# A running product begun one memory head later, and a weight product made ahead of the last column tile

## The chip, the cores and the metric

The kernel runs on one core of a Trainium2 chip. The metric is the device time of one execution in microseconds (us): the median of three runs of the kernel before is 1121.86 us, from 1120.22 to 1121.92. The core has five engines that work through instruction queues of their own: TensorE (PE; its weight loads are shown apart as PEld), VectorE (DVE), ScalarE (ACT), GpSimd (POOL) and SyncE (SP), which issues the loads here.

## What is computed

One hybrid decoder layer on 512 tokens of width 2048, in float32. A conditioning vector gives shift, scale and gate (adaLN); the normalised input goes through one wide projection whose columns feed two groups; both results go through an output projection, are multiplied by the gate and added to the input.

```python
mod = jax.nn.silu(cf) @ w_ada[l] + b_ada[l]
shift, scale, gate = jnp.split(mod, 3, axis=-1)
h = rmsnorm(h_res, ln_g[l]) * (1.0 + scale[:, None]) + shift[:, None]
p = h @ w_in[l] + b_in[l]
...
y_m = mlstm_group(m_x, m_v, m_o, m_z, m_i, m_f, ...)   # 4 memory heads of 256
y_n = nsa_group(n_q, n_kc, n_vc, n_ks, n_vs, n_kw, n_vw, n_g, n_z, ...)  # attention, 4 groups
y = jnp.concatenate([y_m, y_n], axis=-1) @ w_out[l]
h_res = h_res + gate[:, None] * y
```

A memory head convolves m_x over time, makes q and k from the same 256 columns xc by two weight matrices (`q = xch @ wq`, `k = xch @ wk`), and uses the products q k^T under a decay mask to weight v; the result is normalised and multiplied by a sigmoid of m_o and a silu of m_z.

## The kernel before

Activations lie transposed in SBUF: 16 tiles of 128 columns by 512 tokens. To keep float32 precision each operand is split into a high part and a remainder, and each product is three matmuls (high by high, high by low, low by high). The stages follow each other: adaLN and the first column tiles (to 132 us of the span), projections and compression (to 262), attention in four groups with the projections of later column tiles in between (to about 625), four memory heads (to 940), and the output projection (to the end).

`proj(name)` (L286 to L304) makes one column tile of 128 columns: two loads of 512 KB on SP (L292), four weight splits, and 48 matmuls of 512 columns (L298 to L300). A split (L117 to L128) is a cast on ACT (L123, the name ends in h) and a subtraction (L126, the name ends in l), which POOL does while `pat` is "p" (all of attention and head 0) and DVE while it is "v" (afterwards). The tiles are named mx, mv, mo and mz with a number, two of each for one head: mz2 and mz3 belong to head 1. `head_prep(hd)` makes the mx, mv and mz tiles of a head; `memory_head(hd)` does the rest with the mo tiles. The calls are: head_prep(0), conv(2), conv(3), mz_prep(1), and then memory_head(hd) and head_prep(hd + 1) in turn, so mz3 is the last tile ahead of head 0.

In memory_head the two weight matrices are multiplied with each other first: wqk = wq wk^T, 12 matmuls of 256 columns (L721 to L723). ACT casts the product to ah (L727), DVE makes the remainder al (L728), and 12 matmuls give qk = xc times it (L734 to L736). Then come the scores s, the decay weights, the output h and the mo tiles.

`gate_columns` (L809) is the gate's part of adaLN: 4 runs of 16 steps, each with a load of 256 KB on SP (adag, L814) and one DVE instruction that adds a weighted row block to gacc (L817 for the first step of a run, L819 for the others). It is a generator in the list `side_work`; each proj takes two steps from it after either half of its tile.

The instructions are put in order by a scheduler that works from program order and a timeline of its own, under the limits of slot pools: three slots for loaded weights ("raw"), four each for high parts ("whi", also ah) and remainders ("wlo", also al), two PSUM tiles "sc" shared by attention's scores ss and sw, wqk, qk and s. So what is written early can come late on an engine, and each engine then runs its own queue strictly in that order. The names of attention: ss and sw are scores of the selected and the window branch, ep and ec their exponentials (L549 on ACT, after a reduction L542 on DVE), tps, tpw and tpc transposes on PE, phs, phw and phc casts on ACT, pls and plw remainders on DVE, o the output products (L574, L580, L581). Bias, tanh and product of an mz tile are ym and th (L676, L678 on ACT, L679 on DVE).

Of the kernel before, what the change touches and what calls it, by code (L numbers as in the profile page):

```python
# [10 lines left out]
F32 = mybir.dt.float32  # L11
# [75 lines left out]
def layer_kernel(ctx: ExitStack, tc: tile.TileContext, x, cols, ada, ada_g, w_ko, w_tiles,  # L87
# [198 lines left out]
    def proj(name, tag="pj"):  # L286

        ti = TIDX[name] - NKO
        ps = psb(tag, f"pj_{name}")
        for hf in range(2):  # L290
            raw = raw_tile(f"w_{name}_{hf}")
            nc.sync.dma_start(raw, w_tiles[ti, hf])  # L292
            for q in range(2):
                wh, wl = split(raw[:, q * 512:(q + 1) * 512], 512, f"w_{name}_{hf}{q}")
                for j in range(4):
                    k = hf * 8 + q * 4 + j
                    c = slice(j * P, (j + 1) * P)
                    pe.matmul(ps, wh[:, c], hhi[k], start=(k == 0), stop=False)  # L298
                    pe.matmul(ps, wh[:, c], hlo[k], start=False, stop=False)  # L299
                    pe.matmul(ps, wl[:, c], hhi[k], start=False, stop=(k == KT - 1))  # L300
            if side_work:
                for _ in range(SIDE):
                    next(side_work[0], None)
        return ps  # L304

    side_work = []
    SIDE = 2

    def bcol(name):
# [353 lines left out]
        sc.activation(xc[i], acc, AF.Tanh, scale=0.5)  # L663
        ve.scalar_tensor_tensor(xc[i], xc[i], 1.0, acc, op0=ALU.add, op1=ALU.mult)

    def mz_prep(hd):

        tag = ("v", "kh", "kl", "v")[hd]
        shape = [P, 1056] if tag[0] == "k" else [P, 2 * T]
        y2 = na.tile(shape, F32, tag=tag, name=f"ym{hd}", bufs=2)  # L670
        for e in range(2):
            i = 2 * hd + e
            nm = f"mz{i}"
            ps = proj(nm)
            ym[i] = y2[:, e * T:(e + 1) * T]
            sc.activation(ym[i], ps, AF.Identity, bias=bcol(nm))  # L676
            th = tmp(f"th{i}")
            sc.activation(th, ps, AF.Tanh, bias=bhalf[:, TIDX[nm]:TIDX[nm] + 1], scale=0.5)  # L678
            ve.scalar_tensor_tensor(ym[i], th, 1.0, ym[i], op0=ALU.add, op1=ALU.mult)  # L679

    def mv_prep(hd):
        vh = na.tile([P, 1056], F32R, tag="kh", name=f"mvh{hd}", bufs=2)[:, :1032].rearrange("p (a b) -> p a b", b=258)
        vl = na.tile([P, 1056], F32R, tag="kl", name=f"mvl{hd}", bufs=2)[:, :1032].rearrange("p (a b) -> p a b", b=258)
        ve.tensor_copy(vh[:, :, 256:258], ones[:, 0:8].rearrange("p (a b) -> p a b", b=2))
        ve.tensor_copy(vl[:, :, 256:258], zero[:, 0:8].rearrange("p (a b) -> p a b", b=2))
        for e in range(2):
            nm = f"mv{2 * hd + e}"
            ps = proj(nm)
            vr = tmp(f"vr_{nm}")
            sc.activation(vr, ps, AF.Identity, bias=bcol(nm))  # L690
            tp = psb("tp", f"vtp_{nm}")
            for t in range(NT):
                pe.transpose(tp[:, t * P:(t + 1) * P], vr[:, t * P:(t + 1) * P], ident)
            tv = tp.rearrange("p (t d) -> p t d", d=P)
            c = slice(e * P, (e + 1) * P)
            sc.copy(vh[:, :, c], tv)
            ve.tensor_sub(vl[:, :, c], tv, vh[:, :, c].bitcast(F32))
        return vh, vl

    def memory_head(hd, vh, vl):  # L700
        def btile(name):
            return na.tile([P, 640], F32R, tag="bias", name=f"{name}{hd}", bufs=4)
        def etile(name):
            return na.tile([P, T], F32R, tag="ep", name=f"{name}{hd}", bufs=8)
        xh, xl = [etile(f"xh{e}") for e in range(2)], [etile(f"xl{e}") for e in range(2)]
        for e in range(2):
            sc.copy(xh[e], xc[2 * hd + e])
            ve.tensor_sub(xl[e], xc[2 * hd + e], xh[e].bitcast(F32))

        wt = []  # L710
        for w in range(2):
# [14 lines left out]
        s = 1.0 / 64  # L726
        sc.activation(ah, ps, AF.Copy, scale=s)  # L727
        ve.scalar_tensor_tensor(al, ps, s, ah.bitcast(F32), op0=ALU.mult, op1=ALU.subtract)  # L728
        qh, ql = [etile(f"qh{e}") for e in range(2)], [etile(f"ql{e}") for e in range(2)]
        for e in range(2):  # L730
            ps = psb("sc", f"qk{hd}{e}")
            for d in range(2):
                c = slice(d * 256 + e * P, d * 256 + (e + 1) * P)
                pe.matmul(ps, ah[:, c], xh[d], start=(d == 0), stop=False)  # L734
                pe.matmul(ps, ah[:, c], xl[d], start=False, stop=False)
                pe.matmul(ps, al[:, c], xh[d], start=False, stop=(d == 1))  # L736
            sc.copy(qh[e], ps)
            ve.tensor_sub(ql[e], ps, qh[e].bitcast(F32))
        rb = psb("ms", f"rb{hd}")
# [57 lines left out]
    def head_prep(hd):  # L797
# [2 lines left out]
            conv(2 * hd + 1)  # L800
        vv = mv_prep(hd)
        if hd != 1:
            mz_prep(hd)
        return vv


# [33 lines left out]
    vv = head_prep(0)  # L840
    conv(2)
    conv(3)
    mz_prep(1)
    for hd in range(MH):
        memory_head(hd, *vv)
        if hd == 0:
            pat[0] = "v"
            side_work.append(gate_columns())
        if hd + 1 < MH:
            vv = head_prep(hd + 1)  # L850
# [224 lines left out]
```

## Time and profile before

| what | value |
|---|---|
| runs | 1121.86, 1120.22, 1121.92 us |
| the profiled execution | 1121.27 us |
| its span, first to last instruction | 1119.5 us |
| mean granted clock of PE | 0.996 of 2.4 GHz |
| PE busy / PEld busy | 1091.5 us (98%) / 904.8 us (81%) |
| DVE / ACT / POOL busy | 692.9 / 547.2 / 207.8 us |
| chain that ended last, share on PE | 93% |

The profile is one execution. Its times run from the first instruction. A busy time of an engine in a window tells how much it worked there, a wait of an engine names the instruction that it was released by, and a timeline row gives start and length of one instruction. Instructions overlap a little in an engine, so the cost of one in a row of many is the distance between two starts.

### The profile page before, as it was taken

How to read it: one execution, taken by the hardware profiler on the slowest of the kernel's cores; microseconds unless marked ns; L12 is line 12 of the kernel's file. 1: busy time of each engine (PE TensorE's matmuls, PEld its weight loads, DVE VectorE, ACT ScalarE, POOL GpSimd, SP SyncE). 2: the span in 40 equal slices, each digit the busy share in tenths (PEclk: the TensorE clock that was granted, in tenths of full speed). 3: DMA queues.
4: the chain of work that ended last, by engine and by line, in shares of the span. 5: the costliest groups of instructions: out<-in, count | busy, mean ns of one | idle time of the engine just before them, and what ended most of it. 6: DMA issues, size and time to landing. Idle time of an engine off the chain costs nothing.

```text
span 1119.5 us, 18333 instructions
## 1 busy us (share of the span) xinstructions
PE 1091.5 (98%) x6754; PEld 904.8 (81%) x6754; DVE 692.9 (62%) x1739; ACT 547.2 (49%) x1235; POOL 207.8 (19%) x192
## 2 busy tenths in 40 slices
PE   5999999999999999999999899999999999999997
PEld 4777788888888887888788688888888888888896
DVE  6767466226667658666866985588568367445273
ACT  6333452346666668666656744333433264323242
POOL 1000300433335335333532320000010000000000
PEclk9999999999999999999999999999999999999999
DMA  9999424231211211121122443148426222443334
GB/s 375 406 403 379 158 95 135 92 132 60 72 57 57 75 58 58 57 76 57 57 67 66 151 137 108 66 165 277 133 76 207 95 76 84 142 149 131 108 113 160
DMA packets 49362, 150.30 MB, mean 134 GB/s; under 512 B 5876, under 2 KB 7796, under 8 KB 48760
## 3 DMA queue, kind: packets, MB, share of 16 engines
q1 hardware_dynamic: 49272, 149.13, 38.4%
q8 instruction: 53, 0.87, 0.3%
q14 instruction: 37, 0.30, 0.1%
HBM read 144.91 MB, written 4.19 MB: 133 GB/s over the span
## 4 chain that ended last, share of the span: by engine, by line
PE 93%; DVE 3%; ACT 2%; DMA 1%; issue 0%; POOL 0%; ACTq 0%; POOLq 0%; SPq 0%; DVEq 0%
PE ko L263 7%; PE po L945 5%; PE po L946 5%; PE po L947 5%; PE pj_mx L298 3%; PE pj_mx L299 3%; PE pj_mv L300 3%; PE pj_mv L298 3%; PE pj_mx L300 3%; PE pj_mv L299 3%; PE pj_q L298 3%; PE pj_mz L298 3%; PE pj_q L300 3%; PE pj_q L299 3%; PE pj_mz L299 3%; PE pj_mz L300 3%
## 5 line engine op out<-in xcount | busy, mean ns | idle before, releaser
L549 ACT ACTIVATE ep<-ep,nm 128x512 f32<-128x512 f32 (+3 forms) x128 | 71.4, 559 | 28.3 <-DVE nm L542 27.6
L780 POOL TENSOR_TENSOR sm<-sm,mhalf 128x1 f32<-128x1 f32 x16 | 12.0, 760 | 250.3 <-DVE sm L779 149.3
L819 DVE SCALAR_TENSOR_TENSOR gacc<-adag,sil,gacc 128x512 f32<-128x512 f32 x60 | 48.3, 807 | 6.5 <-DMA adag<-in_dram 5.8
L542 DVE CUSTOM_DVE_ANT_0 ep<-sw,bias 128x512 f32<-128x512 f32 (+3 forms) x64 | 29.8, 484 | 19.8 <-PE sw L617 12.4
L223 ACT ACTIVATE hhi<-xts,md 128x512 fp32r<-128x512 f32 x16 | 13.1, 817 | 57.9 <-DVE md L213 57.9
L542 DVE CUSTOM_DVE_ANT_0 ep<-ss,bias 128x512 f32<-128x512 f32 (+3 forms) x64 | 30.5, 486 | 17.4 <-PE tps L568 11.5
L562 DVE TENSOR_SCALAR ep<-ep,ff 128x512 f32<-128x512 f32 (+3 forms) x80 | 36.8, 508 | 0.6
L197 DVE SCALAR_TENSOR_TENSOR acc<-ada,sil,acc 128x256 f32<-128x256 f32 x75 | 36.1, 481 | 1.6
L579 DVE TENSOR_TENSOR pls<-tps,phs 128x512 fp32r<-128x512 f32 x40 | 27.2, 686 | 15.1 <-ACT phs L578 14.6
L907 POOL TENSOR_TENSOR rf<-rf,mhalf 128x1 f32<-128x1 f32 x4 | 2.2, 550 | 177.5 <-ACT tz L900 162.1
L579 DVE TENSOR_TENSOR plw<-tpw,phw 128x512 fp32r<-128x512 f32 x40 | 27.1, 682 | 7.4 <-ACT phw L578 7.1
L529 POOL TENSOR_SCALAR bias<-ct 128x640 f32<-128x640 f32 x16 | 29.6, 1854 | 3.2 <-DVE nm L542 2.2
L206 PEld LDWEIGHTS gp<-ada,cb 128*32 128x32 f32 x1328 | 20.1, 109 | 11.6 <-issue 6.4
L578 ACT CAST phw<-tpw 128x512 fp32r<-128x512 f32 x40 | 22.5, 581 | 11.7 <-PE tpw L568 9.3
L578 ACT CAST phs<-tps 128x512 fp32r<-128x512 f32 x40 | 23.0, 582 | 9.5 <-PE o L574 5.0
L549 ACT ACTIVATE ec<-ec,nm 128x32 f32<-128x32 f32 x64 | 20.2, 315 | 14.6 <-DVE nm L542 14.3
L560 ACT ACTIVATE ep<-ep,ff 128x512 f32<-128x512 f32 (+3 forms) x48 | 23.6, 553 | 7.5 <-DVE ff L554 7.2
L568 PE MATMUL tpw<-ct,ep 128*128 128x128 f32 x160 | 25.7, 272 | 0.1
L568 PE MATMUL tps<-ct,ep 128*128 128x128 f32 x160 | 25.5, 273 | 0.1
L206 PE MATMUL gp<-ada,cb 128*32 128x64 f32 x1328 | 25.6, 221 | 0.0
L568 PEld LDWEIGHTS tps<-ct,ep 128*128 128x128 f32 x160 | 20.1, 140 | 5.8 <-DVE ep L562 0.7
L549 ACT ACTIVATION_READ_ACCUMULATOR ep<-ep,nm 128x1 f32 x128 | 24.2, 189 | 0.0
(1097 smaller groups left out, 3800.1 us busy)
## 6 DMA issues: line engine op xcount, KB each, us to landing
ada<-in_dram SPq DMA_DIRECT2D x64, 512.0 KB, 7.5
adag<-in_dram SPq DMA_DIRECT2D x64, 256.0 KB, 3.9
wo<-in_dram SPq DMA_DIRECT2D x32, 512.0 KB, 3.3
w_q<-in_dram SPq DMA_DIRECT2D x16, 512.0 KB, 3.5
w_mx<-in_dram SPq DMA_DIRECT2D x16, 512.0 KB, 3.5
w_mv<-in_dram SPq DMA_DIRECT2D x16, 512.0 KB, 3.5
w_mz<-in_dram SPq DMA_DIRECT2D x16, 512.0 KB, 3.6
w_mo<-in_dram SPq DMA_DIRECT2D x16, 512.0 KB, 3.5
```

Of the source, the lines that this page charges most:

```text
L263: pe.matmul(ko_ps[j], (wl if p == 1 else wh)[:, c], (hlo if p == 2 else hhi)[k], start=(k == 0 and p == 0), stop=(k == KT - 1 and p == 2))
L298: pe.matmul(ps, wh[:, c], hhi[k], start=(k == 0), stop=False)
L299: pe.matmul(ps, wh[:, c], hlo[k], start=False, stop=False)
L300: pe.matmul(ps, wl[:, c], hhi[k], start=False, stop=(k == KT - 1))
L542: ve.tensor_tensor_reduce(dst, src, bs, -0.125, 3.0e38, ALU.add, ALU.min, nm[:, c:c + 1])
L549: sc.activation(tiles[hd], tiles[hd], AF.Exp, bias=nm[:, 4 * br + hd:4 * br + hd + 1], scale=-1.0, accum_out=zz[:, 4 * br + hd:4 * br + hd ...
L568: pe.transpose(tp[0:rows, hd * P:(hd + 1) * P], srcs[hd], ident)
L579: ve.tensor_sub(pl[0:rows, :], tp[0:rows, :], ph[0:rows, :].bitcast(F32))
L819: ve.scalar_tensor_tensor(acc, raw, w, acc, op0=ALU.mult, op1=ALU.add)
L945: pe.matmul(pss[i][:, :cn], yh[k][:, t], wh[:, c], start=f0, stop=False)
L946: pe.matmul(pss[i][:, :cn], yh[k][:, t], wl[:, c], start=False, stop=False)
L947: pe.matmul(pss[i][:, :cn], yl[k][:, t], wh[:, c], start=False, stop=l0)
```

## The change

Two things are edited. The generator of the gate's running product is appended to the side work after head 1 instead of after head 0, so its 64 steps are taken by the tiles of heads 2 and 3. And the weight product of a head is a function of its own, `weight_product(hd)`, which is called ahead of the last column tile that precedes the head: for head 0 ahead of mz3, for head 1 ahead of mv3, for heads 2 and 3 ahead of mz5 and mz7. What uses it, the qk matmuls, is ordered behind the last matmul of the last projection by `tc.issue_after`. In the new kernel the line numbers from L301 on are one higher, from L700 on they differ more.

```diff
-                    pe.matmul(ps, wl[:, c], hhi[k], start=False, stop=(k == KT - 1))
+                    last_proj[0] = pe.matmul(ps, wl[:, c], hhi[k], start=False, stop=(k == KT - 1)).ins
...
-    def mz_prep(hd):
+    def mz_prep(hd, head=None):
...
+            if e == 1 and head is not None:
+                weight_product(head)
             ps = proj(nm)
...
             nm = f"mv{2 * hd + e}"
+            if e == 1 and hd == 1:
+                weight_product(1)
             ps = proj(nm)
...
+    aqk = {}
+
+    def weight_product(hd):
...
         sc.activation(ah, ps, AF.Copy, scale=s)
         ve.scalar_tensor_tensor(al, ps, s, ah.bitcast(F32), op0=ALU.mult, op1=ALU.subtract)
+        aqk[hd] = ah, al
...
+        ah, al = aqk.pop(hd)
+        before = last_proj[0]
         qh, ql = [etile(f"qh{e}") for e in range(2)], [etile(f"ql{e}") for e in range(2)]
         for e in range(2):
             ps = psb("sc", f"qk{hd}{e}")
-            for d in range(2):
...
+            with tc.issue_after(before):
+                for d in range(2):
...
-            mz_prep(hd)
+            mz_prep(hd, hd if hd else None)
...
-    mz_prep(1)
+    mz_prep(1, 0)
     for hd in range(MH):
         memory_head(hd, *vv)
         if hd == 0:
             pat[0] = "v"
+        if hd == 1:
             side_work.append(gate_columns())
```

The scheduler turns this into another order on each engine. On PE, at the end of mz2 (pj_mz_6837; hhi and hlo are the activations), the kernel before goes straight into mz3 (pj_mz_6910) and takes attention's rows in between:

```order
L299 MATMUL pj_mz_6837<-hlo_1880,w_mz_11h 128x512
L300 MATMUL pj_mz_6837<-hhi_1879,w_mz_11l 128x512
L298 MATMUL pj_mz_6910<-hhi_347,w_mz_00h 128x512
L299 MATMUL pj_mz_6910<-hlo_348,w_mz_00h 128x512
L300 MATMUL pj_mz_6910<-hhi_347,w_mz_00l 128x512
L298 MATMUL pj_mz_6910<-hhi_457,w_mz_00h 128x512
L299 MATMUL pj_mz_6910<-hlo_458,w_mz_00h 128x512
L300 MATMUL pj_mz_6910<-hhi_457,w_mz_00l 128x512
L298 MATMUL pj_mz_6910<-hhi_559,w_mz_00h 128x512
L299 MATMUL pj_mz_6910<-hlo_560,w_mz_00h 128x512
L300 MATMUL pj_mz_6910<-hhi_559,w_mz_00l 128x512
L606 MATMUL ss_5979<-kh_5285,q_q_1_0_5591 128x288
```

The changed kernel has, in the same place, attention alone (the last rows of mz2, then ss, o and tpw):

```order
L299 MATMUL pj_mz_6837<-hlo_1880,w_mz_11h 128x512
L300 MATMUL pj_mz_6837<-hhi_1879,w_mz_11l 128x512
L607 MATMUL ss_5979<-kh_5285,q_q_1_0_5591 128x288
L608 MATMUL ss_5979<-kl_5286,q_q_1_0_5591 128x288
L607 MATMUL ss_5984<-kh_5285,q_q_1_1_5594 128x288
L608 MATMUL ss_5984<-kl_5286,q_q_1_1_5594 128x288
L581 MATMUL o_5802<-phs_5893,v_5366 128x512
L582 MATMUL o_5802<-pls_5894,v_5366 128x512
L569 MATMUL tpw_5920<-ct,ep_5807 128x128
L569 MATMUL tpw_5920<-ct,ep_5808 128x128
```

Here 48 matmuls of mz3 have left the stretch in which attention's last two query blocks are done. They stand behind the weight product (wqk) and the first output products of the last block:

```order
L720 MATMUL wqk_6922<-wqk01h,wqk00h 128x256
L721 MATMUL wqk_6922<-wqk01l,wqk00h 128x256
L722 MATMUL wqk_6922<-wqk01h,wqk00l 128x256
L569 MATMUL tpw_6067<-ct,ep_5968 128x128 x2
L575 MATMUL o_5964<-phc_6030,vcmp 128x512
L581 MATMUL o_5964<-phs_6040,v_5366 128x512
L582 MATMUL o_5964<-pls_6041,v_5366 128x512
L298 MATMUL pj_mz_6939<-hhi_347,w_mz_00h 128x512
L299 MATMUL pj_mz_6939<-hlo_348,w_mz_00h 128x512
L300 MATMUL pj_mz_6939<-hhi_347,w_mz_00l 128x512
```

In the kernel before, the weight product came behind the whole of mz3; now mz3 (pj_mz_6939) comes behind the product.

On ACT at the same place, the kernel before has its weight cast of mz3 early and after the last exponentials ah and the casts of mo0:

```order
L676 ACTIVATE ym_6836<-pj_mz_6910,ct 128x512
L678 ACTIVATE th_6980<-pj_mz_6910,bhalf 128x512
L549 ACTIVATE ep_6102,zz_6097<-ep_6102,nm_6096 128x128
L707 CAST xh_6984<-xc_6366 128x512
L549 ACTIVATE ep_6102,zz_6097<-ep_6102,nm_6096 128x128
L578 CAST phw_6083<-tpw_6078 128x512
L727 ACTIVATE ah_7016<-wqk_7003 128x512
L123 CAST w_mo_00h<-w_mo_0_7189 128x512
L123 CAST w_mo_01h<-w_mo_0_7189 128x512
```

The changed kernel has mz3's first cast right behind ah:

```order
L737 CAST xh_7013<-xc_6366 128x512
L550 ACTIVATE ep_6102,zz_6097<-ep_6102,nm_6096 128x128 x2
L679 ACTIVATE ym_6836<-pj_mz_6837,ct 128x512
L681 ACTIVATE th_6907<-pj_mz_6837,bhalf 128x512
L550 ACTIVATE ep_6102,zz_6097<-ep_6102,nm_6096 128x128
L726 ACTIVATE ah_6935<-wqk_6922 128x512
L123 CAST w_mz_00h<-w_mz_0_6940 128x512
L123 CAST w_mz_01h<-w_mz_0_6940 128x512
```

All exponentials of attention, ym and th of mz2 and ah now stand ahead of the cast that mz3's first matmul reads.

On ACT where head 2 begins, the kernel before ends the last tile (ym, th), makes ah and goes on with the casts of mo4:

```order
L123 CAST wqk20h<-wqk_8479 128x512
L123 CAST wqk21h<-wqk_8485 128x512
L676 ACTIVATE ym_8299<-pj_mz_8386,ct 128x512
L678 ACTIVATE th_8468<-pj_mz_8386,bhalf 128x512
L727 ACTIVATE ah_8504<-wqk_8491 128x512
L123 CAST w_mo_00h<-w_mo_0_8677 128x512
L123 CAST w_mo_01h<-w_mo_0_8677 128x512
```

The changed kernel makes ah after the last tile but one, and the last tile's casts follow it:

```order
L123 CAST wqk21h<-wqk_8335 128x512
L679 ACTIVATE ym_8242<-pj_mz_8243,ct 128x512
L681 ACTIVATE th_8326<-pj_mz_8243,bhalf 128x512
L726 ACTIVATE ah_8354<-wqk_8341 128x512
L123 CAST w_mz_00h<-w_mz_0_8359 128x512
L123 CAST w_mz_01h<-w_mz_0_8359 128x512
```

The cast w_mz_00h, which the last tile's first matmul reads, has moved from a place ahead of the weight product to one behind ah; head 3 has the same rows, head 1 has them with mv in place of mz.

## Rows read from the trace of the kernel before

**Rows 1.** Page: busy time, share of the span and instructions of each engine.
```profile
PE 1091.5 (98%) x6754; PEld 904.8 (81%) x6754; DVE 692.9 (62%) x1739; ACT 547.2 (49%) x1235; POOL 207.8 (19%) x192
```

**Rows 2.** Windows: length, busy us per engine PE to POOL, granted clock, DMA.
```profile
598.40:613.00 14.60, 14.60 (x79) 12.29 (x78) 9.01 (x33) 7.55 (x23) 4.39 (x4) 1.00 0.34 108
613.00:621.30 8.30, 7.97 (x48) 6.50 (x47) 6.33 (x40) 7.67 (x30) 0.00 (x0) 1.00 0.14 36
623.49:626.90 3.41, 1.18 (x6) 0.56 (x4) 3.41 (x8) 3.41 (x10) 0.00 (x0) 1.00 0.54 157
626.90:630.30 3.40, 3.09 (x8) 1.99 (x8) 3.40 (x7) 2.42 (x7) 3.39 (x3) 0.50 0.26 77
665.00:940.00 275.00, 274.04 (x1329) 226.92 (x1327) 174.77 (x361) 107.61 (x205) 10.78 (x18) 1.00 0.39 128
```

**Rows 3.** PE's waits, 623.35 to 665 us, then to 940: total, times, longest.
```profile
PE o L580 <- ACT phw L578: 2.2, 1, 2.2
PE h L770 <- DVE p1l L761: 1.0, 1, 1.0
PE s L754 <- DVE ql L738: 0.5, 1, 0.5
PE pj_mo L300 <- POOL w_mo_00l L126: 0.3, 1, 0.3
...
PE qk L734 <- ACT ah L727: 0.9, 2, 0.5
```

**Rows 4.** Timeline of PE: start, us, engine, line, operation, [idle before it, releaser].
```profile
598.42 0.40 PE L298 MATMUL pj_mz<-hhi,w_mz_00h 128*128 128x512 f32 x1
598.65 0.39 PE L299 MATMUL pj_mz<-hlo,w_mz_00h 128*128 128x512 f32 x1
...
625.83 0.50 PE L580 MATMUL o<-phw,v 128*128 128x512 f32 x1 [2.23 <-ACT phw L578]
...
628.92 0.63 PE L298 MATMUL pj_mo<-hhi,w_mo_00h 128*128 128x512 f32 x1
629.35 0.63 PE L299 MATMUL pj_mo<-hlo,w_mo_00h 128*128 128x512 f32 x1
```

**Rows 5.** Timeline of ACT at the end of attention.
```profile
598.45 0.62 ACT L123 CAST w_mz_11h<-w_mz 128x512 fp32r<-128x512 f32 x1
...
620.84 0.40 ACT L549 ACTIVATE ep<-ep,nm 128x128 f32<-128x128 f32 x1
...
621.24 0.40 ACT L549 ACTIVATE ep<-ep,nm 128x128 f32<-128x128 f32 x1
...
621.62 0.68 ACT L676 ACTIVATE ym<-pj_mz,ct 128x512 f32<-128x512 f32 x1
622.19 0.68 ACT L678 ACTIVATE th<-pj_mz,bhalf 128x512 f32<-128x512 f32 x1
```

**Rows 6.** Timeline of DVE, then of POOL, in the first half of head 0.
```profile
623.13 0.87 DVE L562 TENSOR_SCALAR ep<-ep,ff 128x128 f32<-128x128 f32 x4
...
628.51 1.55 DVE L819 SCALAR_TENSOR_TENSOR gacc<-adag,sil,gacc 128x512 f32<-128x512 f32 x1
...
632.17 0.74 DVE L819 SCALAR_TENSOR_TENSOR gacc<-adag,sil,gacc 128x512 f32<-128x512 f32 x1
632.83 0.28 DVE L562 TENSOR_SCALAR ep<-ep,ff 128x128 f32<-128x128 f32 x1
...
626.91 1.36 POOL L126 TENSOR_TENSOR w_mo_00l<-w_mo,w_mo_00h 128x512 fp32r<-128x512 f32 x1 [4.71 <-ACT w_mo_00h L123]
```

**Rows 7.** Timeline of PE, ACT and DVE where head 3 begins.
```profile
897.56 0.28 PE L723 MATMUL wqk<-wqk31h,wqk30l 128*128 128x256 f32 x1
897.68 0.39 PE L740 MATMUL rb<-rw,dsel 128*128 128x512 f32 x1
898.53 0.51 PE L734 MATMUL qk<-xh,ah 128*128 128x512 f32 x1 [0.46 <-ACT ah L727]
...
897.88 0.60 ACT L727 ACTIVATE ah<-wqk 128x512 fp32r<-128x512 f32 x1 [0.16 <-PE wqk L723]
898.37 0.61 ACT L123 CAST w_mo_00h<-w_mo 128x512 fp32r<-128x512 f32 x1
...
898.56 0.68 DVE L728 SCALAR_TENSOR_TENSOR al<-wqk,ah 128x512 fp32r<-128x512 f32 x1
899.16 0.68 DVE L126 TENSOR_TENSOR w_mo_00l<-w_mo,w_mo_00h 128x512 fp32r<-128x512 f32 x1
```

More of the change, by code (lines that the diff above doesn't have):

```diff
@@ L306, in layer_kernel @@
     side_work = []
+    last_proj = [None]
     SIDE = 2
@@ L698, in mv_prep @@
         return vh, vl
[L700 to L708, printed above, removed]
+    aqk = {}
+    def weight_product(hd):
         wt = []
@@ L728, in memory_head, with btile, etile @@
         ve.scalar_tensor_tensor(al, ps, s, ah.bitcast(F32), op0=ALU.mult, op1=ALU.subtract)
+        aqk[hd] = ah, al
+    def memory_head(hd, vh, vl):
+        def btile(name):
+            return na.tile([P, 640], F32R, tag="bias", name=f"{name}{hd}", bufs=4)
+        def etile(name):
+            return na.tile([P, T], F32R, tag="ep", name=f"{name}{hd}", bufs=8)
+        xh, xl = [etile(f"xh{e}") for e in range(2)], [etile(f"xl{e}") for e in range(2)]
+        for e in range(2):
+            sc.copy(xh[e], xc[2 * hd + e])
+            ve.tensor_sub(xl[e], xc[2 * hd + e], xh[e].bitcast(F32))
+        ah, al = aqk.pop(hd)
+        before = last_proj[0]
         qh, ql = [etile(f"qh{e}") for e in range(2)], [etile(f"ql{e}") for e in range(2)]
@@ L731, in memory_head @@
             ps = psb("sc", f"qk{hd}{e}")
-            for d in range(2):
[L733 to L736, printed above, removed]
+            with tc.issue_after(before):
+                for d in range(2):
+                    c = slice(d * 256 + e * P, d * 256 + (e + 1) * P)
+                    pe.matmul(ps, ah[:, c], xh[d], start=(d == 0), stop=False)
+                    pe.matmul(ps, ah[:, c], xl[d], start=False, stop=False)
+                    pe.matmul(ps, al[:, c], xh[d], start=False, stop=(d == 1))
             sc.copy(qh[e], ps)
```

## The prediction

> **What bounds the kernel now.** I read the busy table first: TensorE (PE) is busy 98% of the span [rows 1], so a change gains only where PE waits and loses wherever a new wait is put in front of it. Next I read the windows around the place that is edited. Before 621.3 us and from 665 to 940 us PE is busy in all but a few tenths to one microsecond of each window; between 623.49 and 626.90 it works 1.18 of 3.41 us, and in the next 3.4 us its granted clock is 0.50 instead of 1.00, which is 1.2 GHz instead of 2.4 [rows 2]. The waits name what ends this hole: ScalarE's (ACT) cast phw, 2.2 us, then the first split of w_mo on GpSimd (POOL) 0.3, and in the same head 0.5 and 1.0 behind subtractions of VectorE (DVE); in the three later heads together PE waits 0.9 us, twice for the cast ah of the weight product [rows 3]. So the handover from attention to head 0 holds 2.2 + 0.3 + 0.5 + 1.0 = 4.1 us of waiting. The timeline gives the cost of the low clock: matmuls of 512 columns start 0.43 us apart at 628.92 instead of 0.23 at 598.42 [rows 4]; the eight instructions of that window run 1.5 us longer than they would at the full clock. Everything that could be won in the stretch is 5.6 us, and 0.9 more in the heads.
>
> **What stays the same.** The same matmuls, casts, splits, loads and gate steps are issued as before; no transfer is added. The sum therefore has only waits in it. It is made against the profiled execution, 1121.27 us, which lies 0.6 us under the median of 1121.86.
>
> **Part 1, the handover's waits go: -5.6 us.** In the new order the 48 matmuls of the tile mz3 stand behind the attention tail and in front of the twelve products qk and of mo0. Eleven microseconds of matmuls (48 x 0.23, [rows 4]) then cover ah, its remainder al, the splits of w_mo and the last casts of attention, for which PE waits now. I take all of the 4.1 + 1.5 us; between 4 and 5.6 are plausible. The gate's running product leaves this stretch but for four of its 64 DVE steps (the new order has adag_0 to adag_3 still there). A step costs DVE 0.66 us from start to start when undisturbed [rows 6]. PE waits for DVE twice here, both counted above, so nothing more comes of it. In heads 2 and 3, where the 60 other steps go, DVE is busy 174.77 of 275.00 us [rows 2], so their 60 x 0.66 = 40 us fit beside PE's work: nothing in the sum. Their loads go past SP's loads of w_mz for the last tile, which are queued behind them but issued well ahead of need: nothing.
>
> **Part 2, the attention tail loses its cover: +6.4 us (5 to 8).** This is the term that decides. Now mz3's matmuls fill PE while the last two query blocks of attention go back and forth between ACT, DVE and PE. In the new order they come only after them, because mz3's first weight cast stands on ACT behind ah, and ah behind the whole queue of attention's exponentials. What PE has to do before mz3's third matmul (the first that needs a POOL split): its busy time from 598.40 to 621.30 is 14.60 + 7.97 = 22.6 us [rows 2]; less mz3's 11.0; less 1.1 for three output products (0.23 each) and four transposes (0.1 each) that now come later; plus twelve weight-product matmuls at 0.12 us [rows 7] and two of mz3, 1.9 together: 12.4 us. What ACT has to do before ah: it was busy 7.55 + 7.67 = 15.2 us in that stretch [rows 2]; less three weight casts that move out (3 x 0.5) and two casts of probabilities that now follow ah (1.0); plus ym and th of mz2 (2 x 0.57), the second xh (0.5) and three exponentials of 0.4 with their reads, which now stand in front of it [rows 5]: 15.2 - 2.5 + 2.8 = 15.5 us. ACT will not work without gaps, since each exponential waits for a score product and its reduction. The row nearest to the new stretch is the window from 613.00, with attention alone on ACT: 7.67 of 8.30, or 92% [rows 2]. At that share ah starts at 598.4 + 15.5/0.92 = 615.2. Then ah 0.5, the cast of w_mz_00h 0.5 and its POOL split 1.3 [rows 5, 6]: mz3's third matmul starts at 617.5. PE has been idle 617.5 - 598.4 - 12.4 = 6.7 us, against 0.3 before. With ACT at 100% this is 5, at 85% some 8. DVE is no later than this: it was busy 9.01 + 6.33 = 15.3 us in the old stretch [rows 2], which holds gate, rescaling and split work that now follows ah, and 15.3 is already under the 16.8 that I give ACT.
>
> **Part 3, the clock after the new hole: +1.5 us (0 to 3).** The idle time is bunched just ahead of mz3. The only like place in the trace is the hole at 623.49, and after it the clock fell to 0.50 for 3.4 us [rows 2], 1.5 us of cost. I take the same once; the scattered waits of the tail may bring it a second time, or the fall may lie in time in which PE waits anyway.
>
> **Part 4, DVE behind POOL: +0.5 us (0 to 2.5).** Three POOL splits of mz3, 1.3 us each, now lie from 616 to 620 beside DVE's gate steps, rescalings and probability splits, which attention's last output products wait for. From th's end at 614.8 to the split pls, DVE has two rescalings of four tiles, two gate steps, ym, al, some reciprocals and pls itself, each 0.6 to 0.9 us [rows 6, 7], 5 us together: pls is ready at 619.8 if nothing disturbs it. A gate step beside a POOL split took 1.55 us, undisturbed 0.74 [rows 6], so each POOL split may delay DVE by 0.8 us, 2.4 in all: 622.2. PE gets to the product with pls after some twenty matmuls of mz3, at 622.3, or at 623.8 with the low clock. The two are nearly level, hence the small value. The Trainium skill's page "SBUF — State Buffer", section "Who interferes with whom", says more: a DVE instruction with two SBUF inputs is fully blocked for the whole of a GpSimd instruction that reads SBUF. By that rule DVE would lose 3 x 1.3 = 3.9 us, an estimate, pls would come at 623.7, this term would be 1.9 at the full clock and the total 1129.4. The one gate step that the trace shows beside a POOL split lost 0.8 us, so the trace agrees that there is a delay and not with its size, and the rule stays out of the sum.
>
> **Part 5, heads 1 to 3: +3.4 us (1.9 to 4).** In these heads the weight product now stands right before the last column tile on PE, and on ACT the tile's first cast stands behind ah, on DVE its first split behind al. Head 3 shows the lengths: the last product matmul starts at 897.56 and the next instruction at 897.68; ah starts at 897.88 and the cast behind it 0.5 later; al starts at 898.56, the next split 0.6 later [rows 7]. So the tile can start when the cast ends, 898.37 + 0.5 = 898.9, and its third matmul when the split ends, 899.16 + 0.6 = 899.8. PE is free at about 897.8 (the small product rb has moved among the others), waits 1.1, does two matmuls, 0.46, and waits 0.4 again: 1.5 us, where it waits 0.5 now [rows 3]. That is +1.1 in head 3, +1.3 in head 2, where one gate step stands between ym and al, and +1.0 in head 1, which has no wait now and four transposes to fill part of it. Before, the twelve qk and the first mo matmuls were there with splits ready beforehand; that cover is gone.
>
> **Sum.** -5.6 + 6.4 + 1.5 + 0.5 + 3.4, plus 0.3 for small waits left in head 0, is +6.5: 1127.8 against the profiled run, 1128.4 against the median. I say 1128.0.
>
> **The rivals.** (a) *Faster.* The tail needs no cover: ACT reaches ah by about 609.5, so that mz3's splits are there when PE comes, and in the heads the cast overtakes in time. Part 2 is then 1, part 5 0.5, parts 3 and 4 nothing: -5.6 + 1 + 0.5 + 0.3 = -3.8, some 1117.5. For it speaks that ACT and DVE are idle 7 and 5.6 of the 14.60 us from 598.40 [rows 2]; against it that the 15.5 us of ACT work stand in order ahead of ah, and that idle time was already taken out. It decides at ah's start: before 610 us it holds. Chance 0.12. (b) *Same.* ACT works without gaps (5.1), no new fall of the clock, heads at their low end: -5.6 + 5.1 + 1.9 + 0.2 = +1.6, 1122.9. Chance 0.20. (c) *Much slower.* ACT at 85%, the clock falls twice, DVE late: -5.6 + 7.8 + 3 + 2.5 + 3.4 + 0.5 = +11.6, 1132.9. Chance 0.12. (d) *The change does not do what it says.* It does so in part: four gate steps stay in the handover, 2.4 us of DVE time, but ACT and not DVE ends the wait there, so this alters none of the cases.
>
> **How the numbers follow.** The forecast itself (1125 to 1131) has 0.56. With (c), slower has 0.68; (b) gives same 0.20; (a) gives faster 0.12. A measurement of this kernel tells about 0.2%, 2.2 us, from no change, so same means 1119.6 to 1124.1. The range from 1120.0 to 1132.5 takes in (b) whole and (c) in its nearer half, and leaves out (a).
>
> **What would show it.** Part 1: the wait of the output product behind phw and the half-clock window right before head 0's first mo matmuls are gone. Part 2: a wait of pj_mz's first matmul behind w_mz_00h and of its third behind the POOL split, ending near 617, with PE's busy time from 598 to 617 near 12.4 us and ACT's share above 85%. Part 3: a window with a granted clock of 0.50 just after. Part 5: waits of pj_mz and pj_mv for ACT and DVE of 1 to 1.5 us in each of heads 1 to 3. I am wrong if ah comes before 610, if PE's waits from 598 to 665 come to under 4 us, or if the last tiles of heads 1 to 3 start without a wait.

## The result and the profile after

The changed kernel takes 1129.86 us (median of 4 runs, 1128.68 to 1130.36) against 1121.68 us of the kernel before in the same comparison: a ratio of 1.0075, 95% interval 1.0063 to 1.0087, or 8.2 us slower. The forecast was 1128.0 us in a range from 1120.0 to 1132.5, slower with a chance of 0.68. The profiled execution has a span of 1128.6 us, 9.1 more than the one of before, and the total is nearly where it was forecast. It is so because two wrong terms of the sum, one too small a gain and one too small a loss, partly cancel; the sections below take them apart.

The busy table of the changed kernel, the line that answers to [rows 1]:

```profile
PE 1095.1 (97%) x6754; PEld 908.0 (80%) x6754; DVE 690.6 (61%) x1739; ACT 546.8 (48%) x1235; POOL 204.7 (18%) x192
```

PE is busy 3.6 us more than before and the span is 9.1 us longer, so 5.5 us are new idle time. The other 3.6 us are longer busy time; some 2.5 of them are twelve matmuls in head 2, which start 0.43 us apart instead of 0.23 (part 5 below).

PE's waits of the changed kernel, first from 590 to 665 us, then to 800, then to 945 (columns: total, times, longest):

```profile
PE pj_mz L298 <- ACT w_mz_00h L123: 2.9, 1, 2.9
PE pj_mz L300 <- POOL w_mz_00l L126: 0.8, 1, 0.8
...
PE pj_mz L300 <- DVE w_mz_00l L126: 3.0, 1, 3.0
PE pj_mz L298 <- ACT w_mz_00h L123: 1.2, 1, 1.2
PE pj_mv L298 <- ACT w_mv_00h L123: 0.8, 1, 0.8
...
PE pj_mz L298 <- ACT w_mz_00h L123: 1.2, 1, 1.2
```

All waits of [rows 3] are gone: phw, w_mo_00l, ql and p1l in the handover and head 0, ah in heads 2 and 3. In their place stand waits of the last column tile: 2.9 and 0.8 us in the handover, 0.8 in head 1, 1.2 and 3.0 in head 2, 1.2 in head 3. Four more waits up to 665 us, of 0.2 to 0.4 us each, are not shown.

Windows of the handover and head 0 and, last, of head 2 (columns as in [rows 2]):

```profile
598.40:613.00 14.60, 13.14 (x83) 10.38 (x81) 13.50 (x69) 12.80 (x47) 0.52 (x1) 1.00 0.19 54
...
617.50:625.00 7.50, 7.35 (x26) 5.88 (x27) 5.58 (x11) 2.10 (x6) 4.40 (x5) 0.77 0.23 72
...
635.00:665.00 30.00, 30.00 (x159) 25.67 (x158) 18.06 (x57) 15.74 (x36) 8.74 (x10) 1.00 0.17 51
...
789.76:793.17 3.41, 3.41 (x8) 2.73 (x9) 1.81 (x3) 0.00 (x0) 0.00 (x0) 0.50 0.36 96
```

From 598.40 to 613.00 ACT works 12.80 us where it worked 7.55 before, and from 635 to 665 PE works all 30.00. In these stages the clock is low twice: in part of the window from 617.50, whose granted clock is 0.77, and in the one from 789.76, where it is 0.50. The second is new.

Where the time went can be read from the starts of tiles that both programs reach with nearly the same work done:

| first matmul of | before, us | after, us | difference |
|---|---|---|---|
| mv2 (end of head 0) | 666.49 | 667.97 | +1.5 |
| mx4 (end of head 1) | 725.73 | 726.82 | +1.1 |
| mx6 (end of head 2) | 829.04 | 836.55 | +7.5 |
| output projection (end of head 3) | 930.73 | 939.85 | +9.1 |
| end of the span | 1119.5 | 1128.6 | +9.1 |

Handover and head 0 cost 1.5 us, head 1 nothing, head 2 6.4 and head 3 1.6. In head 1 the later gate gains what the product costs: the stretch from mv2 to mx4 takes 59.2 us before, 57.2 in the experiment with the later gate and the product moved for head 0 alone, and 58.9 here. About half a us of these differences is work that only changed its head: PE sums the gate's columns in four short groups, and with the later gate the first leaves head 1 and the last one falls at the end of head 3, which takes 0.5 us longer with the later gate alone. Head 2 is the place that was mis-sized: the forecast had 1.3 there.

### The profile page after: what moved, and what is told of

The parts are those of the page before. It is cut to its first block, busy times and chain, and to the rows that moved or that the text cites. A ratio compares the mean times of both kernels' runs of the same rounds, so it can differ in the third digit from the quotient of the medians.

```text
span 1128.6 us, 18325 instructions
## 1 busy us (share of the span) xinstructions
PE 1095.1 (97%) x6754; PEld 908.0 (80%) x6754; DVE 690.6 (61%) x1739; ACT 546.8 (48%) x1235; POOL 204.7 (18%) x192
## 4 chain that ended last, share of the span: by engine, by line
PE 91%; DVE 3%; DMA 2%; ACT 2%; issue 1%; SPq 0%; POOL 0%; ACTq 0%; POOLq 0%; DVEq 0%
PE ko L263 7%; PE po L959 5%; PE po L961 5%; PE po L960 5%; PE pj_mx L298 3%; PE pj_mo L300 3%; PE pj_mx L299 3%; PE pj_mo L298 3%; PE pj_mo L299 3%; PE pj_mx L300 3%; PE pj_q L298 3%; PE pj_q L300 3%; PE pj_q L299 3%; PE pj_mz L300 2%; PE pj_mz L298 2%; PE pj_mz L299 2%
## 5 line engine op out<-in xcount | busy, mean ns | idle before, releaser
L832 DVE SCALAR_TENSOR_TENSOR gacc<-adag,sil,gacc 128x512 f32<-128x512 f32 x60 | 45.9, 765 | 9.4 <-DMA adag<-in_dram 8.7
L563 DVE TENSOR_SCALAR ep<-ep,ff 128x512 f32<-128x512 f32 (+3 forms) x80 | 36.8, 508 | 0.5
```

The source lines that it names most:

```text
L832: ve.scalar_tensor_tensor(acc, raw, w, acc, op0=ALU.mult, op1=ALU.add)
```

## The experiments

Each kernel was timed in rounds beside the kernel before on the same chip; the ratio is to that kernel, which had 1121.65 to 1121.76 us in these comparisons.

**The gate's running product alone.** In the kernel before, one line moves:

```diff
         if hd == 0:
             pat[0] = "v"
+        if hd == 1:
             side_work.append(gate_columns())
```

> The kernel before with the gate's running product begun one head later and nothing else. Theory A (the loss of the changed kernel in head 2, 6.6 us between two tiles' starts, needs both edits: gate steps waiting for their loads on VectorE, and the last tile's first split queued behind them): head 2 keeps its twelve qk matmuls as cover, so no wait over 0.6 us there; the hole behind phw in the handover stays; the waits of 0.5 and 1.0 us in head 0 shrink. 1119.5 to 1122.0 us. Theory B (the weight product's place alone makes the loss): no change, 1121 to 1122. Theory C (the later gate alone makes it, by loads that crowd heads 2 and 3): 5 to 6 us slower, about 1127.

Measured: 1119.41 us, ratio 0.9976 (0.9967 to 0.9985), 2.2 us faster. PE's waits from 598 to 667 us:

```profile
PE o L580 <- ACT phw L578: 2.2, 1, 2.2
PE pj_mo L300 <- POOL w_mo_00l L126: 0.5, 1, 0.5
```

The waits of 0.5 and 1.0 us behind DVE [rows 3] are gone, the hole behind phw is as before, and head 2 has only its 0.5 us for ah. What theory A expected of this kernel holds, with a time 0.1 us under its range, and C falls: the later gate is a gain by itself. B's figure of no change is missed by 1.6 us, but its core, that the product's place makes the loss, is not touched by this run. The gain is more than the 1.5 us of the two listed waits, although the low clock behind the hole lasts longer here (granted clock 0.66 from 625 to 635 us, 0.83 before). By tile starts the kernel is 1.1 us ahead of the one before at mv2 (665.35) and 2.5 at mx4 (723.23), so part of the gain lies in head 1.

**The weight product alone.** In the changed kernel the generator is appended after head 0 again.

```diff
         if hd == 0:
             pat[0] = "v"
-        if hd == 1:
             side_work.append(gate_columns())
```

> The changed kernel with the gate's running product begun after head 0 as before, so the weight product's move alone. Theory A: the handover costs the same net 1 to 2 us, heads 1 and 3 about 1.6 us each, head 2 some 1.6 instead of 6.6 us, unless gate steps now sit ahead of al in head 1: 1125 to 1127 us. Theory B: all of the loss stays, about 1130. Theory C: nothing of the 6.6 us, and the rest small: 1123.

Measured: 1137.24 us, ratio 1.0137 (1.0121 to 1.0152), 15.6 us slower. No theory had this; B, by which all of the loss stays, is the nearest. PE's longest wait and one for ot, both up to 667 us, its wait in head 2, and three rows of DVE in head 0 (vtp_mv are the transposes of an mv tile, ot is attention's output on its way out of PSUM):

```profile
PE vtp_mv L698 <- DVE pls L580: 2.7, 1, 2.7
...
PE o L575 <- DVE ot L634: 0.7, 1, 0.7
...
PE pj_mz L300 <- DVE w_mz_00l L126: 3.0, 1, 3.0
...
625.54 3.36 DVE L832 SCALAR_TENSOR_TENSOR gacc<-adag,sil,gacc 128x512 f32<-128x512 f32 x3
...
630.19 2.12 DVE L832 SCALAR_TENSOR_TENSOR gacc<-adag,sil,gacc 128x512 f32<-128x512 f32 x2 [1.29 <-DMA adag<-in_dram]
632.22 0.68 DVE L580 TENSOR_TENSOR plw<-tpw,phw 128x512 fp32r<-128x512 f32 x1
```

The wait of 3.0 us in head 2 is here too, with the gate begun early, and again a gate step that waited for its load (2.36 us) stands in front of al: theory A is wrong in that the late gate is needed for it. The 64 steps take sixteen column tiles, so with either start some of them lie at the border to head 2. And the handover is 5 us worse than in the changed kernel (mv2 starts at 673.05): three gate steps in a row, 3.36 us, and two more, which waited 1.29 us for a load, sit on DVE ahead of the probability split plw at 632.22, and PE waits for such splits and for ot. So the two edits are tied: the product's move makes DVE's queue in the handover critical, and the gate's move takes steps out of it: 20 of the 64 begin before 667 us here, as in the kernel before, and 4 in the changed kernel. The other 44 lie in heads 2 and 3 with either start. Moved together they cost 8.2, the product without the gate 15.6.

**The weight product moved for head 0 alone**, heads 1 to 3 as before, gate late:

```diff
             nm = f"mv{2 * hd + e}"
-            if e == 1 and hd == 1:
-                weight_product(1)
...
-            mz_prep(hd, hd if hd else None)
+            mz_prep(hd)
...
+        if hd not in aqk:
+            weight_product(hd)
         ah, al = aqk.pop(hd)
```

> The changed kernel with the weight product moved for head 0 alone; heads 1 to 3 make it where they did before. All theories: mz3's first cast still comes behind ah, so the waits of 2.9 and 0.8 us ahead of mz3 stay. Theory A: heads 1 to 3 cost nothing; what remains is the handover's net loss, 1 to 2 us as the start of the tile mv2 showed it: 1122.5 to 1124 us. The forecast's own account (net 3.1 us in the handover) would give 1125. Theory C: 1128.

Measured: 1121.59 us, ratio 0.9996 (0.9988 to 1.0005). PE's waits in the handover, and behind the dots in head 2:

```profile
PE pj_mz L298 <- ACT w_mz_00h L123: 2.9, 1, 2.9
PE pj_mz L300 <- POOL w_mz_00l L126: 0.7, 1, 0.7
...
PE qk L747 <- ACT ah L724: 0.5, 1, 0.5
```

The handover's waits are those of the changed kernel, head 2 is that of the kernel before. The total lies 0.9 us under the lowest expectation (1122.5). Against the gate alone (1119.41) the product of head 0 costs 2.2 us; heads 1 to 3 add the other 8.3 (1129.86 - 1121.59). Between the tile starts of this kernel and the changed one head 1 takes 57.20 and 58.85 us (+1.65), head 2 103.63 and 109.73 (+6.1), head 3 102.16 and 103.30 (+1.1).

**The weight product between the two halves of the last tile**, so that half of the tile's splits and matmuls are ahead of it:

```diff
-    def proj(name, tag="pj"):
+    def proj(name, tag="pj", mid=None):
...
+            if hf == 0 and mid is not None:
+                weight_product(mid)
...
-            if e == 1 and head is not None:
-                weight_product(head)
-            ps = proj(nm)
+            ps = proj(nm, mid=head if e == 1 else None)
```

> The changed kernel with the weight product made between the two halves of the last column tile instead of ahead of it, for all four heads; gate as in the changed kernel. Half of the tile's splits are then ahead of ah on ScalarE and half of its matmuls lie in the attention tail again, the other 24 cover ah. If the loss comes from the tile's splits standing behind ah and al, the waits for w_mz_00h and w_mz_00l go in the handover and in heads 1 to 3, and the gain that was aimed at (up to 5.6 + 0.9 us) shows: 1116 to 1119 us. Rival: the waits only move to the third split, w_mz_10h and its remainder, with the same length: 1126 to 1130.

Measured: 1123.87 us, ratio 1.0016 (1.0007 to 1.0024): 6.0 us better than the changed kernel and 2.2 slower than before. PE's waits in the handover and in head 2:

```profile
PE o L584 <- DVE pls L582: 2.4, 1, 2.4
...
PE pj_mz L298 <- ACT w_mz_10h L123: 1.0, 1, 1.0
```

Both expected totals are missed, and of the waits each expectation had half. Those for w_mz_00h and w_mz_00l are gone, and with them the low clock in head 2 (granted clock 1.00 from 780 to 800 us); a wait of 1.0 us for the third cast (w_mz_10h, in head 1 w_mv_10h), which now stands behind ah, is in each of heads 1 to 3, and in the handover PE waits 2.4 us for DVE's split pls. So the waits follow the order of the splits around ah, and this order is no way to the gain.

**The gate without its loads.** In the changed kernel each run of the gate loads its first block and uses it in all 16 steps:

```diff
-                raw = na.tile([P, T], F32, tag="q", name=f"adag{n}_{k}", bufs=QB)
-                nc.sync.dma_start(raw, ada_g[n, k])
+                if k == 0:
+                    raw = na.tile([P, T], F32, tag="q", name=f"adag{n}_{k}", bufs=QB)
+                    nc.sync.dma_start(raw, ada_g[n, k])
```

> The changed kernel in which each of the gate's four runs loads only its first block and uses it in all 16 steps: the 64 VectorE steps stay, 60 of the 64 gate loads are left out. Theory D (in head 2 al and w_mz_00l stand on VectorE behind gate steps that wait for late loads): the wait of 3.0 us of pj_mz for w_mz_00l in head 2 falls under 1 us and the low clock behind it goes, 4 to 5.5 us less than the changed kernel's 1129.9: 1124.5 to 1126. Theory E (the queue of al, w_mz_00l and plain gate steps is enough, no load matters): wait of 2 us or more stays, 1128 to 1130.

Measured: 1127.12 us, ratio 1.0045 (1.0032 to 1.0057), 2.7 us less than the changed kernel. PE's wait in head 2, and DVE's rows there:

```profile
PE pj_mz L298 <- ACT w_mz_00h L123: 1.2, 1, 1.2
...
781.80 4.18 DVE L833 SCALAR_TENSOR_TENSOR gacc<-adag,sil,gacc 128x512 f32<-128x512 f32 x6
...
787.55 0.69 DVE L727 SCALAR_TENSOR_TENSOR al<-wqk,ah 128x512 fp32r<-128x512 f32 x1 [0.30 <-ACT ah L726]
```

The wait for w_mz_00l is gone, al starts 0.6 us after the start of ah instead of 3.5 (788.42 behind 784.88 in the changed kernel), and from the first product matmul to the qk matmuls head 2 takes 14.4 us (785.06 to 799.45) instead of 19.8, as long as head 3. From mx4 to mx6 it takes 104.30 us, 5.4 less than the changed kernel and 0.7 more than the kernel with the product moved for head 0 alone. That is theory D's size, and E's wait of 2 us or more did not stay. But the run changes two things: no step waits for a load, and the scheduler puts six steps in a row ahead of ah and none between ym and al. By the changed kernel's rows (part 5) the load is 1.5 us of the wait and two gate steps are 0.66 each, so D has the larger part and E is not quite excluded. The total missed its range by 1.1 us at the upper end, since steps that wait for no load are taken earlier by the scheduler and crowd the handover again: 16 begin before 667 us instead of 4, and mv2 starts 1.0 us later, counted from the same weight product.

**The last tile's remainders on GpSimd ahead of head 2.** `pat` is "p" for the tile mz5:

```diff
             if e == 1 and head is not None:
                 weight_product(head)
+                if head == 2:
+                    pat[0] = "p"
             ps = proj(nm)
+            if head == 2:
+                pat[0] = "v"
```

> The changed kernel with the remainders of the last tile ahead of head 2, and of the weight product made with it only as far as the order of the code takes them, on GpSimd instead of VectorE. Theories D and E: the split no longer queues behind gate steps, the third matmul waits 0.9 us (a split of 1.3 less two matmuls) instead of 3.0, no low clock: 1125 to 1127 us. Theory F (the wait there is for the weight load, not for VectorE's queue): 3.0 us stay, 1130.

Measured: 1126.49 us, ratio 1.0042 (1.0029 to 1.0055). PE's waits in head 2, and the split on POOL:

```profile
PE pj_mz L298 <- ACT w_mz_00h L123: 1.2, 1, 1.2
PE pj_mz L300 <- POOL w_mz_00l L126: 1.1, 1, 1.1
...
787.53 1.74 POOL L126 TENSOR_TENSOR w_mz_00l<-w_mz,w_mz_00h 128x512 fp32r<-128x512 f32 x1 [52.66 <-ACT w_mz_00h L123]
```

The third matmul waits 1.1 us instead of 3.0, so the weight had long been loaded and DVE's queue was what held it: F falls. The time is within the range. One detail was not expected: in the profiled execution the clock fell here too, behind waits of 1.2 and 1.1 us. That execution was the slowest of five (1128.99 us, the others 1123.96 to 1127.15), so what the low clock costs in the median is not known.

**Less work on ScalarE ahead of ah.** In the kernel with the product moved for head 0 alone, mz2's bias and tanh are held behind the cast phs of the last but one block (`pcopy` holds the casts of probabilities in program order):

```diff
-                sc.copy(ph[0:rows, :], tp[0:rows, :])
+                pcopy.append(sc.copy(ph[0:rows, :], tp[0:rows, :]).ins)
...
+            with tc.issue_after(pcopy[-5]) if hd == 1 and e == 0 else nullcontext():
                 sc.activation(ym[i], ps, AF.Identity, bias=bcol(nm))
```

> The kernel with the weight product moved for head 0 alone (1121.6 us), with mz2's bias and tanh held behind the cast phs of the last but one block: 1.14 us of work leave ScalarE's queue ahead of ah. If that queue sets when mz3 can begin (part 2 of the prediction): ah near 613.9 instead of 615.0, the wait for w_mz_00h 1.8 instead of 2.9 us, in all 1120 to 1121 us. If the wait is set by VectorE or by the last reductions: no change, 1121.6.

Measured: 1120.14 us, ratio 0.9982 (0.9973 to 0.9991); the kernel without the hold had 1121.59, and the two intervals just touch. The rows of ah and of mz3's first matmul:

```profile
614.93 0.57 ACT L726 ACTIVATE ah<-wqk 128x512 fp32r<-128x512 f32 x1
...
616.06 0.76 PE L298 MATMUL pj_mz<-hhi,w_mz_00h 128*128 128x512 f32 x1 [1.75 <-ACT w_mz_00h L123]
```

The wait is 1.75 instead of 2.9 us. This execution reached the end of mz2 0.85 us later than that of the kernel without the hold (last matmul at 599.36 and 598.51), so ah comes 15.6 us behind mz2's end instead of 16.7: the 1.14 us that left ACT's queue. ACT's queue sets when mz3 begins, as part 2 of the prediction has it.

**The hole of the kernel before, taken at its cause.** If ACT's queue holds ah in the changed kernel, it may also hold phw in the kernel before, where bias and tanh of mz2 and mz3 stand in front of phw [rows 5]. Three kernels start from the one with the gate alone (1119.41 us) and hold mz3's bias and tanh behind the last block's cast phs, or both tiles', or mz2's behind phw and mz3's behind phs:

```diff
+            with tc.issue_after(pcopy[-2]) if hd == 1 and e == 1 else nullcontext():
# both:
+            with tc.issue_after(pcopy[-2]) if hd == 1 else nullcontext():
# mz2 behind phw, mz3 behind phs:
+            with tc.issue_after(pcopy[-3 + e]) if hd == 1 else nullcontext():
                 sc.activation(ym[i], ps, AF.Identity, bias=bcol(nm))
```

> The gate-only kernel (1119.4 us) with the bias and tanh of mz3 on ScalarE held behind the last block's cast phs, which takes 1.14 us of work out of ScalarE's queue ahead of phw, ah and the first cast of mo0. If that queue makes the hole of 2.2 us in the handover: wait behind phw near 1.1 us, a shorter low clock: 1117 to 1118.5. If the hole is made by the transposes or by VectorE: no change, 1119.4.

Measured: 1116.00 us, ratio 0.9947 (0.9934 to 0.9959), 1.0 us under the expected range. The wait that was 2.2 us:

```profile
PE o L581 <- ACT phw L579: 1.1, 1, 1.1
```

> The same with mz2's bias and tanh held too: 2.28 us leave ScalarE's queue ahead of phw. The hole goes as a whole if the queue makes it, and so does the low clock behind it, 3 to 4 us together: 1115.5 to 1117. Against it: mo0 takes the PSUM tile that mz2's bias and tanh set free, so mo0 starts later, and a new wait of 1 to 2 us ahead of mo0 would leave 1118 to 1120.

Measured: 1117.31 us, ratio 0.9961 (0.9947 to 0.9974), 0.3 us over the range. The wait for phw is gone; a wait for DVE's split plw is what is left, and mo0 starts at 629.32 us, 2.7 later than with mz3's alone held, as the objection had it:

```profile
PE o L582 <- DVE plw L580: 1.3, 1, 1.3
```

> Between the two kernels with held evacuations: mz2's bias and tanh right behind the cast phw that ended the hole, mz3's behind phs. phw comes 2.3 us earlier, so its wait goes; ah and mo0's first cast come 1.1 us earlier, so a wait of about 1 us for ah takes its place, and mo0's PSUM tile is free in time: 1115 to 1116.5 us. If the total queue up to ah and not phw alone decides, it equals the kernel with mz3 alone held, 1116.0.

Measured: 1115.60 us, ratio 0.9944 (0.9931 to 0.9956). PE's wait, ACT's rows, and the window in which the clock had fallen before (granted clock after the five engines' busy times):

```profile
PE qk L736 <- ACT ah L729: 1.1, 1, 1.1
...
623.60 0.57 ACT L579 CAST phw<-tpw 128x512 fp32r<-128x512 f32 x1
624.07 0.69 ACT L678 ACTIVATE ym<-pj_mz,ct 128x512 f32<-128x512 f32 x1
...
625.22 0.59 ACT L729 ACTIVATE ah<-wqk 128x512 fp32r<-128x512 f32 x1
...
625.00:635.00 10.00, 9.11 (x40) 7.18 (x41) 9.82 (x16) 8.45 (x20) 5.34 (x4) 1.00 0.21 67
```

The wait of 2.2 us was made by 2.3 us of bias and tanh that nobody needed yet. With mz3's held it is 1.1; with mz2's behind phw it passes to ah, 1.1; in both the total is about 1116, so the queue up to ah decides and not phw alone. The granted clock of the window from 625 us is 1.00 where the gate-only kernel had 0.66. These three kernels beat the kernel before by 4.4 to 6.2 us, of which the later gate gives 2.2, and the changed one by 12.5 to 14.3; their intervals overlap, so which hold is best is not settled.

## Why the prediction came out as it did

**Part 1, gain of the handover, forecast -5.6: too small.** Its waits went as foreseen. The size was wrong, by about 1.5 us: mv2 starts 1.5 us later than before, where parts 1 to 4 and the rest sum to +3.1, and parts 2 to 4 came out as forecast or close to it (below). The window of the kernel before that answers to the third one shown of the changed kernel:

```profile
635.00:665.00 30.00, 28.39 (x148) 23.25 (x148) 27.36 (x55) 12.82 (x27) 9.10 (x7) 1.00 0.49 160
```

PE was busy 28.39 of 30.00 us before and 30.00 after. The 1.6 us between them are the two listed waits behind DVE, but PE also got through 159 matmuls instead of 148, and eleven are worth up to 2.5 us at 0.23. So delays of PE in head 0 that are too short to be listed as waits went too; how much they make, no run isolates. With the gate alone the same window has 160 matmuls in 30.00 us, so the sentence that nothing more comes of the gate steps was wrong. Part 1 also took 60 steps as new to heads 2 and 3, where it is 16; the sum had nothing for either.

**Part 2, the tail without cover, forecast +6.4: right in mechanism and place, with two small misses that cancel.** An ACT row and PE's rows of the changed kernel at the end of the tail:

```profile
615.01 0.58 ACT L726 ACTIVATE ah<-wqk 128x512 fp32r<-128x512 f32 x1
...
616.15 0.50 PE L298 MATMUL pj_mz<-hhi,w_mz_00h 128*128 128x512 f32 x1 [2.90 <-ACT w_mz_00h L123]
...
617.65 0.79 PE L300 MATMUL pj_mz<-hhi,w_mz_00l 128*128 128x512 f32 x1 [0.77 <-POOL w_mz_00l L126]
618.24 0.63 PE L298 MATMUL pj_mz<-hhi,w_mz_00h 128*128 128x512 f32 x1
618.67 0.63 PE L299 MATMUL pj_mz<-hlo,w_mz_00h 128*128 128x512 f32 x1
```

ah starts at 615.01 (forecast 615.2), mz3's third matmul at 617.65 (617.5), and the experiment that shortened ACT's queue by 1.14 us moved ah by as much. That the start is met to 0.2 us is in part luck: from 598.40 up to ah ACT worked 14.8 of 16.6 us, 89%, where the forecast had 15.5 us at 92%; the smaller work alone puts ah some 0.7 us earlier, the smaller share 0.5 later. One sign was missed: PE's busy time from 598 to 617 is 14.5 us and not 12.4, so less of the 6.7 us shows as idle time. The other part is in busy time, since a matmul alone is shown with 0.4 to 0.8 us and one in a row costs 0.23.

**Part 3, the clock, forecast +1.5: right.** The rows above show 512-column matmuls 0.43 us apart from 618.24 on, which lasts up to 620.8; the eight matmuls from 617.65 on take 3.5 us, 1.7 more than at 0.23 each.

**Part 4, DVE behind POOL, forecast +0.5: the delay came and cost nothing.** Two POOL splits, DVE's rows beside them (L563 rescales exponentials), and the output product that uses pls:

```profile
616.23 1.37 POOL L126 TENSOR_TENSOR w_mz_00l<-w_mz,w_mz_00h 128x512 fp32r<-128x512 f32 x1 [11.29 <-ACT w_mz_00h L123]
617.56 1.73 POOL L126 TENSOR_TENSOR w_mz_01l<-w_mz,w_mz_01h 128x512 fp32r<-128x512 f32 x1
...
616.38 1.76 DVE L832 SCALAR_TENSOR_TENSOR gacc<-adag,sil,gacc 128x512 f32<-128x512 f32 x1
618.07 2.78 DVE L563 TENSOR_SCALAR ec<-ec,ff 128x32 f32<-128x32 f32 x4
...
621.64 0.69 DVE L580 TENSOR_TENSOR pls<-tps,phs 128x512 fp32r<-128x512 f32 x1
...
624.19 0.39 PE L582 MATMUL o<-pls,v 128*128 128x512 f32 x1
```

The gate step took 1.76 us (0.74 undisturbed) and the four rescalings 2.78 instead of 0.8: 3.0 us of delay against 2.4 forecast. The forecast went by one gate step beside a POOL split; the trace of before has three more in head 0, which took 1.55 to 1.77 us and so lost 0.8 to 1.0. The Trainium skill's rule ("SBUF — State Buffer", section "Who interferes with whom") gave 3.9 as an estimate; the measurement lies between the two. Two of the 3.0 us fell on the rescalings, which have one tile operand, where the prediction took the rule for instructions with two. pls started at 621.64 (forecast ready at 622.2), and PE came for it at 624.19 and for plw 0.45 us later, both times without a wait.

**Part 5, heads 1 to 3, forecast +3.4: mis-sized in head 2.** By tile starts against the kernel with the product moved for head 0 alone, heads 1 and 3 cost 1.65 and 1.1 us (forecast 1.0 and 1.1). Head 2 cost 6.1 where 1.3 was forecast. PE's and DVE's rows there, and ACT's cast:

```profile
786.04 0.50 PE L298 MATMUL pj_mz<-hhi,w_mz_00h 128*128 128x512 f32 x1 [1.19 <-ACT w_mz_00h L123]
...
789.76 0.79 PE L300 MATMUL pj_mz<-hhi,w_mz_00l 128*128 128x512 f32 x1 [2.99 <-DVE w_mz_00l L126]
...
786.49 0.75 DVE L832 SCALAR_TENSOR_TENSOR gacc<-adag,sil,gacc 128x512 f32<-128x512 f32 x1 [1.54 <-DMA adag<-in_dram]
...
787.76 0.74 DVE L832 SCALAR_TENSOR_TENSOR gacc<-adag,sil,gacc 128x512 f32<-128x512 f32 x1
788.42 0.68 DVE L727 SCALAR_TENSOR_TENSOR al<-wqk,ah 128x512 fp32r<-128x512 f32 x1
789.02 0.68 DVE L126 TENSOR_TENSOR w_mz_00l<-w_mz,w_mz_00h 128x512 fp32r<-128x512 f32 x1
...
785.37 0.61 ACT L123 CAST w_mz_00h<-w_mz 128x512 fp32r<-128x512 f32 x1
```

PE waits 1.19 us for the cast, as worked out, and then 2.99 instead of 0.4 for the remainder w_mz_00l. On DVE it stands behind al, al behind a gate step, ym and another gate step, and that one waits 1.54 us for its load; the split itself starts at 789.02, 3.0 us after its cast was done. Behind the wait the clock is down: twelve matmuls of mz5 take 5.3 us, 2.5 more than at 0.23 each. The two waits, less the 0.5 us that PE waited in head 2 before, and these 2.5 us roughly make up the 6.1.

The step that failed is the price of 1.3 for head 2, which put one undisturbed step with its data there between ym and al, and behind it the sentence in part 1 that the gate's loads are issued well ahead of need and cost nothing. The load waited for took 4.5 us to land and others issued shortly before took up to 6.9; DMA was 89% busy from 783 to 786. The late start of the gate is not the reason, since the kernel with the product alone has the same wait. In the kernel without these loads the wait of 3.0 us is gone, with the split on POOL it is 1.1. A second miss was the low clock, which I priced for the handover and not for head 2.

**Rivals.** The faster case needed ah by 609.5; it came at 615.0. The equal case needed heads at their low end, which head 2 excludes. Case (c), 1132.9 us, did not come: ACT was at 89% and not 85, and pls did not hold PE up; a second fall of the clock did come, but in head 2 and not in the tail. Case (d) was judged rightly: four gate steps stayed in the handover, and ACT ended its longest wait. The time lies in the forecast's own band of 1125 to 1131, by two terms that were wrong in opposite directions, part 1 by 1.5 us and part 5 by more.

## What to carry to other kernels

Before work that fills a busy engine's gaps is moved behind something, list what each other engine's queue holds ahead of the moved work's first input: here 15.5 us of ScalarE work ahead of one cast, counted from the trace (14.8 in the run), gave the new hole's place to 0.2 us, with some luck in the share of gaps. A step that is cheap because its data are there is not cheap in a new place: where its load is late, everything queued behind it on the same engine is late too, and that must be priced with the load's landing time. And a hole is best looked at from the queue of the engine that ends it: the bias and tanh of two tiles, which nobody needed yet, stood in front of the cast, and holding them back, with the later gate, won 4.4 to 6.2 of the 6.5 us that the move was after.

## What the runs showed of the hardware

- DVE's four rescalings (one tile operand each, 128x32) took 2.78 us beside POOL's splits and 0.80 in the kernel before without a split beside them, so a DVE instruction with a single tile operand can be slowed too.
- In two pairs of a gate step (two tile operands) and a POOL split, the one that started second was the longer: a step that started 0.15 us behind a split took 1.76 us and the split 1.37 (part 4); in the kernel with remainders on GpSimd a step that started 0.14 us ahead of the split shown there took 0.75 and the split 1.74, part of it beside the DVE instruction that came next. Undisturbed they take 0.74 and 1.28.
- Waits of 1.19 and 1.08 us with two matmuls between them were followed, four matmuls on, by matmuls 0.43 us apart (granted clock 0.62 from 789.3 to 793.5) in the kernel with remainders on GpSimd; a wait of 1.19 us in head 3 of the changed kernel, with none of note behind it, was not, and its window shows 1.00.
